# First block's two mixers: long convolution's taps all as matrix products from stored diagonals, output projection row by row into four PSUM banks

## Chip, cores and metric

The kernel runs on one core of a Trainium2 chip. The metric is the device time of one execution, from the first to the last instruction with the launch around it, in microseconds (us). Lower is better.

## What is computed

A network of two parts on 256 tokens of width 1024, in float32. The first block has two layers; each is a hybrid mixer, a residual sum with a layer norm, a feed-forward net (dense in layer 0, a mixture of eight experts in layer 1) and another layer norm. A second block with three kinds of attention and two more feed-forward nets follows; the change leaves it alone. What matters here, cut from the reference:

```python
def hybrid_mixer(...):
    proj = jnp.einsum('btd,de->bte', x, w_in)
    ...
    o_a = (rms_norm_f32(o_a, gdn_norm_w) * silu(a_gate)) ...    # 384 columns, gated delta rule
    glu_a, glu_b = jnp.split(c_glu, 2, axis=-1)
    u = glu_a * jax.nn.sigmoid(glu_b)
    u = causal_depthwise_conv(u, cnv_dw_w) + cnv_dw_b           # 31 taps, 256 channels
    o_b = jax.nn.silu(layer_norm(u, cnv_ln_g, cnv_ln_b))
    ...                                                         # o_c: 384 columns, attention
    mixed = jnp.concatenate([o_a, o_b, o_c], axis=-1) * mix_scale
    return jnp.einsum('bte,ed->btd', mixed, w_out)              # 1024 x 1024

x = layer_norm(DEEPNORM_ALPHA * x + mix, ln_mix_g[l], ln_mix_b[l])
```

## The kernel before

Tokens stand in two tiles of 128, channels in chunks of 128. Matrix products with weights are done in three pieces to keep float32 accuracy: `load` (L166) fetches a weight block of 1 MB into one of four `raw` buffers, `part` (L169) splits each half of it into a high part `wh` (a copy on ScalarE, L172) and a low part `wl` (a subtraction on VectorE, L174), three such pairs being held at a time, and `mm3` issues three products (L183 to L185) of a faster float32 form. `split_t` transposes activations on TensorE (L267) and splits them in the same way (L277, L278 with a gain). All other products are plain float32 products at L362; the profile shows each of those as two instructions.

`mixer1` (L354) is one layer's mixer. Its last part runs five generators: the inverse of the delta rule's triangular blocks, the `scan` over four chunks of 64 tokens (`g_ws`, `g_S`, `g_o`), the attention `fox` (`f_fl` logits, `f_fpt` transposes, `f_fo` values), `conv`, and `gates`. They are written one after another, but a scheduler that works with its own estimate of every instruction's time sets the order in which the instructions stand on each engine; an engine then works through its own list in that order. PSUM has eight banks: two under the tag `a`, four under `g`, two under `f`.

`conv` (L740) builds the gated input `up` (`cup`, 30 zeros and 256 tokens for each of two channel chunks) and applies 31 taps to each chunk. The nearest 6 taps of a chunk (8 in layer 1) go to TensorE: ScalarE scales the identity by the tap's weights (`dgt`, L756) and a product with it adds the shifted input to the bank `a_conv`. The other 25 (23) are one VectorE instruction each (L762, L764), which multiplies a shifted input by the weights and adds to `ccv`. L765 adds both. Then comes a layer norm over channels, with two products with ones (`f_cmean`, `f_cvar`), and a SiLU (L771 to L784).

`gates` (L787) projects the last 256 gate columns (48 products into `a_pB`), and applies a SiLU in three ScalarE passes. After the five, the convolution's result is scaled and split into chunks 3 and 4 of `mT` (L802, L803), the attention's result is transposed into chunks 5 to 7, and the delta rule's, normed and gated (L810 to L816), into chunks 0 to 2.

The output projection (L823 to L828) takes the 1024 output columns in four blocks of 256. Each block loads all 1024 rows of its columns, sums 48 products of 256 columns into one bank (`proj_b`), and is added to the residual (L826) with its statistics taken (L828), while TensorE goes on with the next block. `moments` (L834) then joins the statistics of both token tiles, takes the reciprocal root on ScalarE, and `layer_norm_T` or `layer_norm_T_first` scales (L850, L851 or L864) and transposes.

Of the kernel before, what the change touches and what calls it, by code (L numbers as in the profile page):

```python
# [9 lines left out]
F32 = mybir.dt.float32  # L10
# [4 lines left out]
AF = mybir.ActivationFunctionType  # L15
ALU = mybir.AluOpType
# [64 lines left out]
FOXC, GLUC = (5, 6, 7), (8, 9)  # L81

PCOLS1 = []
for _l in range(2):
    PCOLS1 += [(f"rowp{_l}", 24), (f"cw{_l}", 36), (f"mix{_l}", 8), (f"gnw{_l}", 1), (f"dww{_l}", 62), (f"dwb{_l}", 2),
               (f"clg{_l}", 2), (f"clb{_l}", 2)]
# [17 lines left out]
class Net:  # L104
# [249 lines left out]
    def mixer1(self, l, x, xT):  # L354
# [6 lines left out]
        def mm(out, lhsT, rhs, start=True, stop=True, **kw):  # L361
            PE.matmul(out, lhsT, rhs, start=bool(start), stop=bool(stop), skip_group_check=True, **kw)  # L362
# [377 lines left out]
        def conv():  # L740
# [9 lines left out]
            near = 31 - (6, 8)[l]  # L750
            dw, db = self.col1(f"dww{l}"), self.col1(f"dwb{l}")
            pc = self.ps("a", "conv").rearrange("p (c n) -> p c n", c=2)
            for c in range(2):
                for j in range(near, 31):
                    dg = mp.tile([P, P], F32, name="dgt", bufs=2)
                    S.activation(dg, ident, AF.Copy, scale=dw[:, c * 31 + j:c * 31 + j + 1])  # L756
                    mm(pc[:, c, :], dg, up[:, c, j:j + T], start=j == near, stop=j == 30)
            for c in range(2):
                for j in range(near):
                    w = dw[:, c * 31 + j:c * 31 + j + 1]  # L760
                    if j == 0:
                        V.tensor_scalar(cv[:, c, :], up[:, c, 0:T], w, db[:, c:c + 1], op0=ALU.mult, op1=ALU.add)  # L762
                    else:
                        V.scalar_tensor_tensor(cv[:, c, :], up[:, c, j:j + T], w, cv[:, c, :], op0=ALU.mult, op1=ALU.add)  # L764
            V.tensor_tensor(cv, cv, pc, op=ALU.add)  # L765
            yield
            ps = self.ps("f", "cmean")
# [5 lines left out]
            ps = self.ps("f", "cvar")  # L773
# [26 lines left out]
        for c in range(2):  # L800
            g = msc[:, 3 + c:4 + c]
            S.activation(mT[0][:, 3 + c, :], cv[:, c, :], AF.Copy, scale=g)  # L802
            V.scalar_tensor_tensor(mT[1][:, 3 + c, :], cv[:, c, :], g, mT[0][:, 3 + c, :].bitcast(F32),  # L803
                                   op0=ALU.mult, op1=ALU.subtract)
        self.split_t("f", mixed, mT, range(5, 8), gains=msc, src0=3)
# [12 lines left out]
        self.dump(f"cv{l}", cv)  # L818


        self.split_t("g", mixed, mT, range(0, 3), gains=msc, src0=0)
        r, st = x, self.new_stats()
        for c in range(4):  # L823
            ps = self.proj_b(A["w_out"][l, c], mT)
            s = slice(c * 256, c * 256 + 256)
            V.scalar_tensor_tensor(r[:, :, s], x[:, :, s], ALPHA, ps, op0=ALU.mult, op1=ALU.add)  # L826
            for t in range(2):
                V.bn_stats(out=st[:, t, c, :], in_=r[:, t, s])  # L828
# [5 lines left out]
    def moments(self, r, st, n):  # L834
        nc = self.nc
        mv, rs = self.ap.tile([P, 2, 2], F32, name="bnmv"), self.ap.tile([P, 2], F32, name="bnrs")
        for t in range(2):
            nc.vector.bn_aggr(out=mv[:, t, :], in_=st[:, t, :n, :])
        self.normed = self.rsqrt(rs, mv[:, :, 1], 1.0, 1e-5)
        return mv, rs  # L840

    def layer_norm_T(self, tag, r, st, rows, n=4):

        V = self.nc.vector
        mv, rs = self.moments(r, st, n)
        xT = self.new_xT()
        for h in range(2):
            s = slice(h * 512, h * 512 + 512)
            for t in range(2):
                V.scalar_tensor_tensor(r[:, t, s], r[:, t, s], mv[:, t, 0:1], rows[:, 0, s], op0=ALU.subtract, op1=ALU.mult)  # L850
                V.scalar_tensor_tensor(r[:, t, s], r[:, t, s], rs[:, t:t + 1], rows[:, 1, s], op0=ALU.mult, op1=ALU.add)  # L851
            self.split_t(tag, r, xT, range(4 * h, 4 * h + 4), src0=4 * h)
        return xT

    def layer_norm_T_first(self, tp, tag, r, st, rows, name, n=4):
# [3 lines left out]
        mv, rs = self.moments(r, st, n)  # L859
        hi, lo = xT = self.new_xT()  # L860
        for h in range(2):
            s = slice(h * 512, h * 512 + 512)
            for t in range(2):
                V.tensor_scalar(r[:, t, s], r[:, t, s], mv[:, t, 0:1], rs[:, t:t + 1], op0=ALU.subtract, op1=ALU.mult)  # L864
# [917 lines left out]
def zeros(*s):  # L1782
    return np.zeros(s, np.float32)


def pack_first(I):
# [6 lines left out]
    out["w_out"] = pack_b(I["w_out"])  # L1793
    cols = {}
    for l in range(2):
# [7 lines left out]
        cols[f"dww{l}"] = I["cnv_dw_w"][l].reshape(31, 2, P).transpose(2, 1, 0).reshape(P, 62)  # L1803
# [54 lines left out]
def build(tc, A, out):  # L1858
    with ExitStack() as ctx:
# [14 lines left out]
        with net.banks(a=2, g=4, f=2), pool("mix1") as net.mp:  # L1874
            rows = net.load_rows(net.mp.tile([P, 2, D], F32, name="rows", tag="lb"), "ln_ffn", 0, 2)
            xT = net.layer_norm_T("g", r, st, rows, 2)
            r, st = net.mixer1(1, r, xT)
# [36 lines left out]
```

## Time and profile before

| | us |
|---|---|
| median of 3 runs | 2170.08 (2164.84 to 2173.29) |
| the profiled execution, its own time | 2177.81 |
| span of its instructions | 2176.0 |
| first mixer's last part, projection included | about 118 to 207 |
| second mixer's last part, projection included | about 521 to 616 |

Times below count from the start of the span. The clock of TensorE is given as a share of its full 2.4 GHz: 1.00, or 0.50 for 1.2 GHz. A matrix product's listed duration holds its way through the array, so successive products overlap; what one costs in a row of them is the distance from start to start.

### The profile page before, as it was taken

The numbers are of one execution on the slowest core, as the hardware profiler recorded it, in microseconds if no ns is written. First come the engines' busy times: TensorE is split into PE (matmuls) and PEld (weight loads), VectorE is DVE, ScalarE is ACT, GpSimd is POOL, SyncE is SP. The second block draws the span as 40 slices with busy tenths as digits, with TensorE's granted clock in tenths as the row PEclk, the third lists the DMA queues.
The fourth block names the chain that finished last, engine by engine and source line by source line (L and its number), as shares of the span: only waits on it lengthen the run. The fifth ranks groups of instructions, "written<-read, shape, count | busy, mean of one in ns | idle before, by whom it ended". The sixth has DMA issues, their size and how long they took to land. (4 is left out here: it accounts for less than half of the span.)

```text
span 2176.0 us, 31850 instructions
## 1 busy us (share of the span) xinstructions
PE 2079.3 (96%) x12770; PEld 1598.7 (73%) x12770; DVE 1295.8 (60%) x1903; ACT 1017.1 (47%) x1445; POOL 12.7 (1%) x27
## 2 busy tenths in 40 slices
PE   8998999899979999999999999999899999999998
PEld 7887999778766565565565565555699988888997
DVE  6767955676666555454564465454555568765444
ACT  6545444464435454444454454443444444644443
POOL 0000000000000000000000000000000000000000
PEclk9979999998889999999999999999999999999999
DMA  6313675422359999999999999999455553444552
GB/s 236 104 44 118 213 258 182 137 90 96 139 178 347 364 406 378 415 415 371 401 372 383 400 389 393 421 417 398 168 192 180 190 183 126 136 164 155 186 183 98
DMA packets 78987, 545.36 MB, mean 251 GB/s; under 512 B 8960, under 2 KB 11272, under 8 KB 13936
## 3 DMA queue, kind: packets, MB, share of 16 engines
q1 hardware_dynamic: 76112, 527.40, 63.8%
q0 software_dynamic: 2720, 15.84, 2.0%
q8 instruction: 103, 1.69, 0.3%
q14 instruction: 52, 0.43, 0.1%
HBM read 536.72 MB, written 6.49 MB: 250 GB/s over the span
## 5 line engine op out<-in xcount | busy, mean ns | idle before, releaser
L174 DVE TENSOR_TENSOR wl<-raw,wh 128x1024 fp32r<-128x1024 f32 (+1 forms) x662 | 798.1, 1217 | 432.3 <-ACT wh L172 420.5
L172 ACT ACTIVATE wh<-raw 128x1024 fp32r<-128x1024 f32 (+1 forms) x662 | 690.7, 1054 | 627.9 <-PE a_pA L184 270.3
L183 PE MATMUL a_pA<-xTh,wh 128*128 128x256 f32 x1456 | 419.0, 289 | 6.2 <-ACT foxqk L620 3.5
L185 PE MATMUL a_pA<-xTh,wl 128*128 128x256 f32 x1456 | 415.5, 286 | 0.8 <-DVE wl L174 0.7
L184 PE MATMUL a_pA<-xTl,wh 128*128 128x256 f32 x1456 | 415.6, 286 | 0.4 <-DVE xTl L278 0.2
L183 PEld LDWEIGHTS a_pA<-xTh,wh 128*128 128x128 f32 x1456 | 280.8, 193 | 14.7 <-ACT foxqk L620 5.6
L184 PEld LDWEIGHTS a_pA<-xTl,wh 128*128 128x128 f32 x1456 | 281.0, 193 | 5.3 <-issue 3.2
L185 PEld LDWEIGHTS a_pA<-xTh,wl 128*128 128x128 f32 x1456 | 280.8, 193 | 3.8 <-issue 2.2
L1033 PE MATMUL a_up<-raw,xef 128*64 128x512 f32 x896 | 213.5, 596 | 0.0
L184 PE MATMUL a_up<-wl,xeh 128*128 128x512 f32 x448 | 180.7, 403 | 0.5 <-DVE wl L174 0.4
L183 PE MATMUL a_up<-wh,xeh 128*128 128x512 f32 x448 | 177.7, 400 | 0.0
L185 PE MATMUL a_up<-wh,xel 128*128 128x512 f32 x448 | 177.3, 396 | 0.0
L1033 PEld LDWEIGHTS a_up<-raw,xef 128*64 128x64 f32 x896 | 65.1, 137 | 127.8 <-issue 122.3
L1038 DVE TENSOR_TENSOR mos<-mos,a_up 128x512 f32<-128x512 f32 x42 | 28.8, 685 | 200.3 <-PE a_up L1033 149.8
L183 PE MATMUL a_pB<-wh,xTh 128*128 128x256 f32 x480 | 141.5, 296 | 5.7 <-ACT glu L620 3.2
L185 PE MATMUL a_pB<-wh,xTl 128*128 128x256 f32 x480 | 138.6, 291 | 1.6 <-DVE xTl L278 1.6
L184 PE MATMUL a_pB<-wl,xTh 128*128 128x256 f32 x480 | 139.8, 292 | 0.0
L1066 PE MATMUL y_y<-raw,mof 128*64 128x512 f32 x448 | 132.8, 602 | 0.7 <-ACT mof L1052 0.7
L184 PEld LDWEIGHTS a_up<-wl,xeh 128*128 128x128 f32 x448 | 84.6, 189 | 34.5 <-issue 11.4
L183 PEld LDWEIGHTS a_up<-wh,xeh 128*128 128x128 f32 x448 | 84.7, 189 | 28.1 <-ACT wh L172 7.3
L185 PE MATMUL acc_acc<-wh,ffl 128*128 128x512 f32 x264 | 102.0, 392 | 0.0
L184 PE MATMUL acc_acc<-wl,ffh 128*128 128x512 f32 x264 | 101.9, 392 | 0.0
(556 smaller groups left out, 2703.2 us busy)
## 6 DMA issues: line engine op xcount, KB each, us to landing
raw<-in_moe_w_dram SPq DMA_DIRECT2D x336, 1024.0 KB, 9.2
raw<-in_ffn_in_dram SPq DMA_DIRECT2D x44, 1024.0 KB, 4.9
raw<-in_ffn_w_dram SPq DMA_DIRECT2D x33, 1024.0 KB, 5.0
raw<-in_w_in_a_dram SPq DMA_DIRECT2D x24, 1024.0 KB, 4.9
raw<-in_ffn_out_dram SPq DMA_DIRECT2D x22, 1024.0 KB, 4.9
raw<-in_w_out_dram SPq DMA_DIRECT2D x12, 1024.0 KB, 4.9
raw<-in_w_in_g_dram SPq DMA_DIRECT2D x12, 1024.0 KB, 4.9
raw<-in_w_in_b_dram SPq DMA_DIRECT2D x6, 1024.0 KB, 5.1
```

The costliest lines, as they stand in the source:

```text
L172: nc.scalar.activation(wh[:, :m], raw[:, o:o + m], AF.Copy)
L174: nc.vector.tensor_tensor(wl[:, :m], raw[:, o:o + m], wh[:, :m].bitcast(F32), op=ALU.subtract)
L183: mm(out, lh, rh, start=start, stop=False, skip_group_check=True)
L184: mm(out, lh, rl, start=False, stop=False, skip_group_check=True)
L185: mm(out, ll, rh, start=False, stop=stop, skip_group_check=True)
L1033: PE.matmul(ps[r], xe[0][:, k0, r], w[:, k * 512:k * 512 + 512], start=k0 == 0, stop=k0 == 7, skip_group_check=True)
L1038: V.tensor_tensor(s, s, pp[1], op=ALU.mult)
L1066: PE.matmul(py[h][r], hf[:, k, r], w[:, j * 1024 + h * 512:j * 1024 + h * 512 + 512], start=b == 0 and k == 0, stop=b == 6 and k == 3, ski ...
```

## The change

All 62 taps of a layer become products on TensorE. Their diagonal matrices are no longer made on the chip: they are prepared beforehand as `w_tap`, four blocks of 1 MB per layer, which go through the same four `raw` buffers as the weights. The VectorE and ScalarE instructions of the taps are gone; the bias is added by two ScalarE copies out of PSUM. The two products of the channel norm take `g` banks in place of `f`. The output projection runs by rows of the weight matrix: a block of 1 MB holds two chunks of 128 rows in all 1024 columns, in the order 5, 6, 7, 3, 4, 0, 1, 2, and each chunk's products, now 512 columns wide, go to four banks that stay open (two token tiles by two column halves). The source writes the last three chunks bank by bank, and the statistics, the root and the scaling token tile by token tile; the second layer's mixer enters through the changed `layer_norm_T` too.

```diff
@@ -79,10 +79,11 @@
+OUT_ROWS = [5, 6, 7, 3, 4, 0, 1, 2]
...
@@ -747,30 +748,23 @@
             V.memset(up[:, :, 0:30], 0.0)
             V.tensor_tensor(up[:, :, 30:], glu[:, 2:4, :], sg, op=ALU.mult)
             yield
-            near = 31 - (6, 8)[l]
-            dw, db = self.col1(f"dww{l}"), self.col1(f"dwb{l}")
+            db = self.col1(f"dwb{l}")
             pc = self.ps("a", "conv").rearrange("p (c n) -> p c n", c=2)
+            for i in range(4):
+                raw = self.load(A["w_tap"][l, i]).rearrange("p (j n) -> p j n", n=P)
+                for n in range(16 * i, min(16 * i + 16, 62)):
+                    c, j = n // 31, n % 31
+                    mm(pc[:, c, :], raw[:, n % 16, :], up[:, c, j:j + T], start=n == 0, stop=n == 61)
             for c in range(2):
-                for j in range(near, 31):
-                    dg = mp.tile([P, P], F32, name="dgt", bufs=2)
-                    S.activation(dg, ident, AF.Copy, scale=dw[:, c * 31 + j:c * 31 + j + 1])
-                    mm(pc[:, c, :], dg, up[:, c, j:j + T], start=j == near, stop=j == 30)
-            for c in range(2):
-                for j in range(near):
-                    w = dw[:, c * 31 + j:c * 31 + j + 1]
-                    if j == 0:
-                        V.tensor_scalar(cv[:, c, :], up[:, c, 0:T], w, db[:, c:c + 1], op0=ALU.mult, op1=ALU.add)
-                    else:
-                        V.scalar_tensor_tensor(cv[:, c, :], up[:, c, j:j + T], w, cv[:, c, :], op0=ALU.mult, op1=ALU.add)
-            V.tensor_tensor(cv, cv, pc, op=ALU.add)
-            yield
-            ps = self.ps("f", "cmean")
+                S.activation(cv[:, c, :], pc[:, c, :], AF.Identity, bias=db[:, c:c + 1])
+            yield
+            ps = self.ps("g", "cmean")
             for c in range(2):
                 mm(ps[:, :T], self.ones, cv[:, c, :], start=c == 0, stop=c == 1)
             for c in range(2):
                 V.scalar_tensor_tensor(cv[:, c, :], ps[:, :T], -1.0 / 256, cv[:, c, :], op0=ALU.mult, op1=ALU.add)
             S.activation(csq, cv, AF.Square)
-            ps = self.ps("f", "cvar")
+            ps = self.ps("g", "cvar")
             for c in range(2):
                 mm(ps[:, :T], self.ones, csq[:, c, :], start=c == 0, stop=c == 1)
             crs = glu[:, 2, :]
@@ -797,12 +791,6 @@
         V.tensor_scalar(msc[:, 0:3], msc[:, 0:3], self.col1(f"gnw{l}"), None, op0=ALU.mult)
         self.emit(inverse(), scan(), fox(), conv(), gates())
         mT = self.new_xT()
-        for c in range(2):
-            g = msc[:, 3 + c:4 + c]
-            S.activation(mT[0][:, 3 + c, :], cv[:, c, :], AF.Copy, scale=g)
-            V.scalar_tensor_tensor(mT[1][:, 3 + c, :], cv[:, c, :], g, mT[0][:, 3 + c, :].bitcast(F32),
-                                   op0=ALU.mult, op1=ALU.subtract)
-        self.split_t("f", mixed, mT, range(5, 8), gains=msc, src0=3)
 
 
         for t in range(2):
@@ -816,52 +804,73 @@
             V.tensor_tensor(mixed[:, t, 0:384], sq, o_sb[:, t, :], op=ALU.mult)
         self.dump(f"mixed{l}", mixed)
         self.dump(f"cv{l}", cv)
-
-
         self.split_t("g", mixed, mT, range(0, 3), gains=msc, src0=0)
+
+
+        self.split_t("g", mixed, mT, range(5, 8), gains=msc, src0=3)
+        for c in range(2):
+            g = msc[:, 3 + c:4 + c]
+            S.activation(mT[0][:, 3 + c, :], cv[:, c, :], AF.Copy, scale=g)
+            V.scalar_tensor_tensor(mT[1][:, 3 + c, :], cv[:, c, :], g, mT[0][:, 3 + c, :].bitcast(F32),
+                                   op0=ALU.mult, op1=ALU.subtract)
+        acc = [self.ps(n, "wo") for n in "ffaa"]
+        last = []
+
+        def out(k, w, t, h, **kw):
+            ts, hs = slice(t * P, t * P + P), slice(h * 512, h * 512 + 512)
+            self.mm3(acc[2 * t + h], mT[0][:, k, ts], mT[1][:, k, ts], w[0][:, hs], w[1][:, hs], **kw)
+
+        for i in range(4):
+            for k, w in zip(OUT_ROWS[2 * i:2 * i + 2], self.weights(A["w_out"][l, i])):
+                if k < 3:
+                    last.append((k, w))
+                    continue
+                for t in range(2):
+                    for h in range(2):
+                        out(k, w, t, h, start=k == OUT_ROWS[0], stop=False)
         r, st = x, self.new_stats()
-        for c in range(4):
-            ps = self.proj_b(A["w_out"][l, c], mT)
-            s = slice(c * 256, c * 256 + 256)
-            V.scalar_tensor_tensor(r[:, :, s], x[:, :, s], ALPHA, ps, op0=ALU.mult, op1=ALU.add)
-            for t in range(2):
-                V.bn_stats(out=st[:, t, c, :], in_=r[:, t, s])
+        for t in range(2):
+            for h in range(2):
+                for k, w in last:
+                    out(k, w, t, h, start=False, stop=k == OUT_ROWS[-1])
+                s = slice(h * 512, h * 512 + 512)
+                V.scalar_tensor_tensor(r[:, t, s], x[:, t, s], ALPHA, acc[2 * t + h], op0=ALU.mult, op1=ALU.add)
+                V.bn_stats(out=st[:, t, h, :], in_=r[:, t, s])
         return r, st
 
     def new_stats(self):
         return self.ap.tile([P, 2, 4, 6], F32, name="bnst")
 
-    def moments(self, r, st, n):
-        nc = self.nc
+    def moments(self, st):
+
         mv, rs = self.ap.tile([P, 2, 2], F32, name="bnmv"), self.ap.tile([P, 2], F32, name="bnrs")
         for t in range(2):
-            nc.vector.bn_aggr(out=mv[:, t, :], in_=st[:, t, :n, :])
-        self.normed = self.rsqrt(rs, mv[:, :, 1], 1.0, 1e-5)
-        return mv, rs
-
-    def layer_norm_T(self, tag, r, st, rows, n=4):
+            self.nc.vector.bn_aggr(out=mv[:, t, :], in_=st[:, t, :2, :])
+            self.normed = self.rsqrt(rs[:, t:t + 1], mv[:, t, 1:2], 1.0, 1e-5)
+            yield t, mv[:, t, 0:1], rs[:, t:t + 1]
+
+    def layer_norm_T(self, tag, r, st, rows):
 
         V = self.nc.vector
-        mv, rs = self.moments(r, st, n)
         xT = self.new_xT()
-        for h in range(2):
-            s = slice(h * 512, h * 512 + 512)
-            for t in range(2):
-                V.scalar_tensor_tensor(r[:, t, s], r[:, t, s], mv[:, t, 0:1], rows[:, 0, s], op0=ALU.subtract, op1=ALU.mult)
-                V.scalar_tensor_tensor(r[:, t, s], r[:, t, s], rs[:, t:t + 1], rows[:, 1, s], op0=ALU.mult, op1=ALU.add)
-            self.split_t(tag, r, xT, range(4 * h, 4 * h + 4), src0=4 * h)
+        for t, mv, rs in self.moments(st):
+            for h in range(2):
+                s = slice(h * 512, h * 512 + 512)
+                V.scalar_tensor_tensor(r[:, t, s], r[:, t, s], mv, rows[:, 0, s], op0=ALU.subtract, op1=ALU.mult)
+                V.scalar_tensor_tensor(r[:, t, s], r[:, t, s], rs, rows[:, 1, s], op0=ALU.mult, op1=ALU.add)
+                if t:
+                    self.split_t(tag, r, xT, range(4 * h, 4 * h + 4), src0=4 * h)
         return xT
 
-    def layer_norm_T_first(self, tp, tag, r, st, rows, name, n=4):
+    def layer_norm_T_first(self, tp, tag, r, st, rows, name):
 
         V, S = self.nc.vector, self.nc.scalar
         g, b = self.col1(name + "g"), self.col1(name + "b")
-        mv, rs = self.moments(r, st, n)
         hi, lo = xT = self.new_xT()
-        for h in range(2):
-            s = slice(h * 512, h * 512 + 512)
-            for t in range(2):
-                V.tensor_scalar(r[:, t, s], r[:, t, s], mv[:, t, 0:1], rs[:, t:t + 1], op0=ALU.subtract, op1=ALU.mult)
+        for t, mv, rs in self.moments(st):
+            for h in range(2):
+                s = slice(h * 512, h * 512 + 512)
+                V.tensor_scalar(r[:, t, s], r[:, t, s], mv, rs, op0=ALU.subtract, op1=ALU.mult)
...
@@ -1790,7 +1799,11 @@
     out["w_in_a"] = pack_a(a)
     out["w_in_b"] = pack_b(w[:, :, W_IN_B])
     out["w_in_s"] = pack_b(w[:, :, W_IN_S], 18)[:, 0]
-    out["w_out"] = pack_b(I["w_out"])
+    taps = zeros(2, 64, P, P)
+    i = np.arange(P)
+    taps[:, :62, i, i] = I["cnv_dw_w"].reshape(2, 31, 2, P).transpose(0, 2, 1, 3).reshape(2, 62, P)
+    out["w_tap"] = np.ascontiguousarray(taps.reshape(2, 4, 16, P, P).transpose(0, 1, 3, 2, 4)).reshape(2, 4, P, 2048)
+    out["w_out"] = pack_rows(I["w_out"].reshape(2, KC, P, D)[:, OUT_ROWS].reshape(2, D, D))
     cols = {}
     for l in range(2):
         cw = I["gdn_conv_w"][l]
```

The order in which instructions now stand differs from the source in places. TensorE in the first mixer's last part, around the second chunk of the scan, before:

```order
L362 MATMUL g_ws<-late 64x128 x3
L362 MATMUL g_o<-late,kq_283 64x128
L362 MATMUL g_o<-late,kq_358 64x128
L362 MATMUL g_o<-late,kq_431 64x128
L362 MATMUL f_fo<-fv,fpT 128x64 x12
L362 MATMUL a_conv<-cup,dgt 128x256 x2
L362 MATMUL g_S<-late,kd_792 64x64 x2
L362 MATMUL g_S<-late,kd_799 64x64 x2
L362 MATMUL g_S<-late,kd_806 64x64 x2
```

The same engine from the third chunk of the scan to the first product of `gates`, now:

```order
L363 MATMUL g_o<-late,AT_537 64x64 x2
L363 MATMUL g_o<-late,AT_554 64x64 x2
L363 MATMUL g_o<-late,AT_571 64x64 x2
L363 MATMUL a_conv<-cup,raw 128x256 x11
L363 MATMUL g_ws<-late 64x128 x3
L363 MATMUL g_o<-late,kq_283 64x128
L363 MATMUL g_o<-late,kq_358 64x128
L363 MATMUL g_o<-late,kq_431 64x128
L363 MATMUL a_conv<-cup,raw 128x256 x11
L363 MATMUL g_o<-late,AT_537 64x64 x2
L363 MATMUL g_o<-late,AT_554 64x64 x2
L363 MATMUL g_o<-late,AT_571 64x64 x2
```

The taps stood singly or in pairs between the scan's steps, with the products of `gates` among them; now they stand in runs of up to 11 (3, 3, 3, 6, 1, 8, 10, 11, 11, 6 in either mixer), and all 48 products of `gates` come after the last run.

ScalarE in the first mixer, from the copy of the `gates` bank on, before (the channel norm's square is L772, its SiLU further down; L735 copies the scan's results):

```order
L790 ACTIVATE gate<-a_pB 128x2x256
L172 ACTIVATE wh<-raw 128x1024
L299 ACTIVATE late<-gate 128x768
L300 ACTIVATE late<-late,bias_294 128x768
L735 ACTIVATE mixed<-g_o 64x384
L301 ACTIVATE late<-late 128x768
L810 ACTIVATE late<-mixed 128x384
L772 ACTIVATE glu<-ccv 128x512
L293 ACTIVATE ors<-ors,bias_524 128x6
L735 ACTIVATE mixed<-g_o 64x384
```

The same engine now, further down in the same chain, as far as the first copies of transposed tiles (L813 scales the convolution's result, L278 splits the transposed tiles):

```order
L302 ACTIVATE late<-late 128x768
L798 ACTIVATE late<-mixed 128x384 x2
L300 ACTIVATE glu<-glu 128x512
L294 ACTIVATE ors<-ors,bias_524 128x6
L301 ACTIVATE glu<-glu,bias_294 128x512
L295 ACTIVATE ors<-ors 128x6
L294 ACTIVATE ors<-ors,bias_524 128x6
L302 ACTIVATE glu<-glu 128x512
L295 ACTIVATE ors<-ors 128x6
L813 ACTIVATE xTh<-ccv,msc 128x256 x2
L278 ACTIVATE xTh<-g_tr,msc 128x256 x6
```

The gate's SiLU stood among the scan's last copies; now it stands behind them, the convolution's SiLU follows it, and all six splits of transposed tiles stand behind both.

VectorE at the end of the first mixer's projection, before:

```order
L826 SCALAR_TENSOR_TENSOR x<-x,a_pB 128x2x256
L828 BN_STATS bnst<-x 128x6 x2
L174 TENSOR_TENSOR wl<-raw,wh 128x1024
L838 BN_AGGR bnmv<-bnst 128x2 x2
L864 TENSOR_SCALAR x<-x,bnmv,bnrs 128x512 x4
```

and now:

```order
L837 SCALAR_TENSOR_TENSOR x<-x,f_wo 128x512 x2
L837 SCALAR_TENSOR_TENSOR x<-x,a_wo 128x512 x2
L838 BN_STATS bnst<-x 128x6 x2
L175 TENSOR_TENSOR wl<-raw,wh 128x1024
L838 BN_STATS bnst<-x 128x6 x2
L848 BN_AGGR bnmv<-bnst 128x2 x2
L873 TENSOR_SCALAR x<-x,bnmv,bnrs 128x512 x4
```

Both token tiles' sums, statistics and roots stand side by side rather than one tile after the other. On TensorE the last chunks of rows stand chunk by chunk through all four banks (two products for one bank, two for the next), so that the four banks close within the last eight products.

## Rows read from the trace of the kernel before

**Rows 1.** The page's first part: busy us, share of the span, instructions.

```profile
PE 2079.3 (96%) x12770; PEld 1598.7 (73%) x12770; DVE 1295.8 (60%) x1903; ACT 1017.1 (47%) x1445; POOL 12.7 (1%) x27
```

**Rows 2.** First mixer by stretches: length, engines' busy us, TensorE's clock, DMA share, GB/s.

```profile
122.20:146.10 23.90, 23.90 (x191) 16.58 (x187) 12.90 (x38) 8.85 (x32) 0.00 (x0) 0.50 0.01 2
146.10:162.30 16.20, 16.20 (x150) 14.65 (x149) 13.74 (x33) 5.68 (x14) 0.00 (x0) 1.00 0.20 66
162.30:175.90 13.60, 9.02 (x81) 7.04 (x81) 10.79 (x23) 9.73 (x21) 0.87 (x2) 1.00 0.00 1
175.90:203.00 27.10, 26.44 (x192) 25.90 (x192) 19.16 (x35) 13.31 (x20) 1.19 (x3) 0.87 0.55 197
```

**Rows 3.** The second mixer in the same view; columns PE, PEld, DVE, ACT, POOL.

```profile
525.00:552.30 27.30, 27.30 (x210) 19.18 (x210) 14.01 (x41) 10.36 (x36) 0.00 (x0) 0.50 0.00 1
573.10:580.50 7.40, 4.81 (x33) 3.46 (x32) 5.92 (x14) 5.17 (x14) 0.49 (x1) 1.00 0.93 352
580.50:608.60 28.10, 25.82 (x192) 24.80 (x192) 14.63 (x26) 9.51 (x14) 0.04 (x1) 0.94 0.71 269
```

**Rows 4.** Taps on TensorE: the tile's view (ns min/median/max), then the timeline (start, us).

```profile
L362 PE MATMUL a_conv<-cup,dgt x56: 377/483/795, 123.0 to 571.3; 128*128 128x256 f32 x56
...
132.23 2.07 PE L362 MATMUL a_conv<-cup,dgt 128*128 128x256 f32 x4
...
149.92 1.03 PE L362 MATMUL a_conv<-cup,dgt 128*128 128x256 f32 x4
```

**Rows 5.** Taps on VectorE, and a VectorE instruction queued among them with its wait.

```profile
L764 DVE SCALAR_TENSOR_TENSOR ccv<-cup,p,ccv x92: 443/477/486, 122.6 to 565.4; 128x256 f32<-128x256 f32 x92
...
129.31 0.69 DVE L661 TENSOR_REDUCE fsx<-f_fl 128x2 f32<-128x512 f32 x1 [4.07 <-PE f_fl L362]
```

**Rows 6.** Timeline of ScalarE and VectorE behind the products of `gates` in the first mixer.

```profile
162.30 0.60 ACT L790 ACTIVATE gate<-a_pB 128x512 f32<-128x512 f32 x1 [2.76 <-PE a_pB L185]
162.79 1.05 ACT L172 ACTIVATE wh<-raw 128x1024 fp32r<-128x1024 f32 x1
163.74 0.83 ACT L299 ACTIVATE late<-gate 128x768 f32<-128x768 f32 x1
...
166.68 0.96 DVE L792 TENSOR_TENSOR gate<-gate,late 128x768 f32<-128x768 f32 x1 [0.27 <-ACT late L301]
...
177.77 0.71 ACT L300 ACTIVATE glu<-glu,bias 128x512 f32<-128x512 f32 x1
...
179.18 0.69 DVE L784 TENSOR_TENSOR ccv<-ccv,glu 128x512 f32<-128x512 f32 x1 [0.79 <-ACT glu L301]
...
179.90 0.91 ACT L802 ACTIVATE xTh<-ccv,msc 128x256 fp32r<-128x256 f32 x2 [0.76 <-DVE ccv L784]
```

**Rows 7.** Timeline of TensorE: 512-column products into four banks (20 starts between), 256-column ones (156).

```profile
254.83 0.39 PE L183 MATMUL acc_acc<-wh,ffh 128*128 128x512 f32 x1
...
259.37 0.39 PE L185 MATMUL acc_acc<-wh,ffl 128*128 128x512 f32 x1
...
184.01 0.28 PE L183 MATMUL a_pB<-wh,xTh 128*128 128x256 f32 x1
...
202.73 0.28 PE L185 MATMUL a_pB<-wh,xTl 128*128 128x256 f32 x1
```

**Rows 8.** Timeline of VectorE and TensorE at the first norm; statistics over 512 columns elsewhere.

```profile
203.04 0.69 DVE L826 SCALAR_TENSOR_TENSOR x<-x,a_pB 128x512 f32<-128x512 f32 x1 [0.56 <-PE a_pB L185]
203.76 0.75 DVE L828 BATCH_NORM_STATS2 bnst<-x 128x6 f32<-128x256 f32 x2
204.44 1.21 DVE L174 TENSOR_TENSOR wl<-raw,wh 128x1024 fp32r<-128x1024 f32 x1
...
206.54 1.92 DVE L864 TENSOR_SCALAR x<-x,bnmv,bnrs 128x512 f32<-128x512 f32 x4 [0.60 <-ACT bnrs L294]
...
207.14 3.70 PE L869 MATMUL a_tr<-call,x 128*128 128x128 f32 x16 [4.13 <-DVE x L864]
...
407.74 0.67 DVE L906 BATCH_NORM_STATS2 bnst<-x 128x6 f32<-128x512 f32 x1
```

More of the change, by code (lines that the diff above doesn't have):

```diff
@@ L81 @@
 FOXC, GLUC = (5, 6, 7), (8, 9)
+OUT_ROWS = [5, 6, 7, 3, 4, 0, 1, 2]
 PCOLS1 = []
 for _l in range(2):
-    PCOLS1 += [(f"rowp{_l}", 24), (f"cw{_l}", 36), (f"mix{_l}", 8), (f"gnw{_l}", 1), (f"dww{_l}", 62), (f"dwb{_l}", 2),
+    PCOLS1 += [(f"rowp{_l}", 24), (f"cw{_l}", 36), (f"mix{_l}", 8), (f"gnw{_l}", 1), (f"dwb{_l}", 2),
                (f"clg{_l}", 2), (f"clb{_l}", 2)]
@@ L1802, in pack_first @@
         cols[f"gnw{l}"] = np.concatenate([I["gdn_norm_w"][l]] * 2)[:, None]
-        cols[f"dww{l}"] = I["cnv_dw_w"][l].reshape(31, 2, P).transpose(2, 1, 0).reshape(P, 62)
         cols[f"dwb{l}"] = chan(I["cnv_dw_b"][l], 2)
@@ L1875, in build @@
             rows = net.load_rows(net.mp.tile([P, 2, D], F32, name="rows", tag="lb"), "ln_ffn", 0, 2)
-            xT = net.layer_norm_T("g", r, st, rows, 2)
+            xT = net.layer_norm_T("g", r, st, rows)
             r, st = net.mixer1(1, r, xT)
```

## The prediction

> **What bounds the kernel now.** Read the engine shares first [rows 1]: TensorE is busy for 96% of the span, so work that is added to it is suspected of lengthening the span until an idle or slowed stretch is found that takes it in. The change works in two places, the last parts of the two mixers, so the next view is the table of stretches for these [rows 2, 3]. It shows three things.
>
> First, from the start of the convolution to the end of the gate's products TensorE has no idle time at all: 23.90 of 23.90 us and 16.20 of 16.20 in the first mixer, 27.30 of 27.30 in the second. VectorE, which carries most of the taps, is busy for 12.90 of the 23.90 us. Second, in the two long stretches TensorE's granted clock is 0.50, that is 1.2 GHz, although it never rests: what it does there are attention logits with 18 and 64 rows and products of 32 and 64 rows and columns, with a few full-size taps among them. Third, in the stretch before the output projection TensorE idles, 13.60 - 9.02 = 4.58 us in the first mixer and 7.40 - 4.81 = 2.59 in the second, and within the projection 27.10 - 26.44 = 0.66 and 28.10 - 25.82 = 2.28 us.
>
> Is it VectorE that holds TensorE back in the long stretch? Then taking the taps away from it would pay. An instruction of the attention that is queued behind taps on VectorE shows the reverse [rows 5]: VectorE had finished its taps and stood idle for 4.07 us, waiting for TensorE's logits. So the last parts of the mixers are bound by TensorE, first by its work at either clock, then by the chain through ScalarE and VectorE that leads to the projection.
>
> **Taps.** 50 taps in the first layer and 46 in the second leave VectorE (0.48 us each [rows 5], hidden beside TensorE) and go to TensorE; 28 diagonals leave ScalarE, hidden too. A tap is two instructions there. One alone takes 0.377 us, four in a row 1.03, so each further one adds (1.03 - 0.377) / 3 = 0.218 us; at half clock (2.07 - 0.795) / 3 = 0.425 [rows 4]. A tap costs 0.436 us or 0.85. With no idle time around them 96 taps add 96 x 0.436 = 41.9 us, 21.8 and 20.1. This is the bulk of the sum. In the new order 9 taps stand ahead of the scan's first state product where 6 stood, so 3 more in either mixer fall into the slow stretch if that stays: 6 x 0.41 = 2.5 us, less what moves out of it; taken as 2.
>
> Is the long stretch still slow? The work that stands there keeps its shape; what is new is a run of three taps for every two or three logits. A run is 1.3 us at full clock, against some 2 to 4 us of small products around it. In the trace two pairs of taps in the same stretch did not lift the clock. I take it that the slow stretches stay about as long, and keep the other end (both vanish, less 23.90 / 2 + 27.30 / 2 = 25.6 us) as a rival.
>
> The Trainium skill, on the page "TensorE: Matmul & The Clock Gate", section "Loop structure matters more than you think", says that it is the loop nest that decides whether matmuls stay warm: issued back to back they keep the full clock. The trace differs here, since 23.90 us without a gap ran at 0.50 [rows 2]; by the page's rule that stretch would not be slow at all, before or after, and the time would be that of the rival "full clock" below.
>
> **The chain to the projection.** All 48 products of the gate now stand behind the last tap, and behind them on ScalarE comes everything that leads to `mT`. The durations are in the trace [rows 6]: copy of the bank 0.60, a weight split that stands next in the queue 1.05, three SiLU passes of at least 0.83 (2.49), VectorE's product 0.96; then, since the convolution's SiLU is queued behind and the transposed splits behind that, three passes of 0.71 (2.13), VectorE's product 0.69, the two scalings 0.91, the first split 0.46. Sum 9.3 us. Between them stand hand-overs and small instructions of the norm, for which I add 2 (from 0 to 4): 11.3 us from the last gate product to the first of the projection. TensorE fills some 2.4 of it (two products of the channel norm, 0.87 like two taps, and transposes), so it idles about 8.9 us. Before it was 4.58 and 2.59, since the gate's products stood between the scan's steps; that is +4.3 and +6.3. The late splits then no longer stall the projection: -0.66 and -2.28. Together +7.7 (from +4 to +13). Who waits for this chain is TensorE alone, with the whole projection queued.
>
> The tap blocks take the four `raw` buffers, so the gate's and the projection's loads start only as runs of taps end. The last of those loads to be needed, rows of the third block, starts at the last tap and has the chain and half the projection to arrive: nothing.
>
> **Projection.** It changes from 192 products of 256 columns to 96 of 512. Start to start these are (202.73 - 184.01) / 156 = 0.120 us and (259.37 - 254.83) / 20 = 0.227 us [rows 7]: 23.0 against 21.8 us, -1.2 each, -2.5 together. The clock dips at its start (0.87 and 0.94 [rows 2, 3]) because of the idle time ahead; this stays.
>
> [...]
>
> **Norm.** Before, 4.1 us pass from the last product to the first transposes (203.0 to 207.14 [rows 8]): one addition 0.69, statistics of two pieces 0.75, a weight split 1.21, the root, the scaling. The new order doesn't take one token tile ahead of the other: four banks close within 2 us, and then four additions (0.6 apart), four statistics of 0.67 and the same split stand in the queue, and the transposes need the third of four scalings (1.92 / 4 apart) instead of the second. That is about 2.8 us more by the rows, but additions and statistics may overlap the last products. I take +2 for each mixer, +4 (from -4, if the halves work as the source writes them, to +8).
>
> **Sum.** 41.9 + 2 + 7.7 - 2.5 + 4 = +53.1 us. The profiled execution of 2177.81 us would take 2231; it lies 7.7 us above the median of the runs, from which I count: 2170.08 + 53.1 = 2223.
>
> **Rivals.**
> *Full clock in the long stretches.* Runs of full-size taps among the logits keep TensorE at 2.4 GHz. For it: in 146.1 to 162.3, with taps and gate products among the same scan, the clock was 1.00 [rows 2]. Against it: 0.50 for 24 and 27 us with taps in them. Price -25.6 and -2: 2196; in one mixer only, about 2210.
>
> *The taps are absorbed: not slower.* TensorE's stream becomes so dense that the clock stays full from the logits to the norm and no idle time is left. The gain is at most 25.6, plus 0.13 x 27.1 + 0.06 x 28.1 = 5.2 in the projections, plus the idle 4.58 + 2.59 + 0.66 + 2.28 = 10.1: 40.9 us, against 41.9 - 2.5 = 39.4 of work. That gives -1.5, 2169. It decides only if all of this is gained; each half-clock stretch of 10 us that stays costs 5. Against it stands the new order, in which the gate's chain has nothing left on TensorE to cover it.
>
> *Bank cycling slows the projection.* The new products would run at half clock throughout, 0.227 x 96 = 21.8 us more in each mixer: 2267. The rows of the feed-forward net speak against it. [...]
>
> **How the numbers follow.** The forecast has 0.62, full clock in one or both long stretches 0.21, absorbed taps 0.08, bank cycling 0.03, something else 0.06. The range for 8 in 10 takes in the full-clock case and the forecast's own bounds: from 2223 - 27.6 - 10 = 2186 to 2223 + 15 = 2238. A measurement of this kernel can tell about 0.5% from no change, 11 us; only the absorbed case and part of the rest end within that, so faster 0.05, same 0.08, slower 0.87.
>
> **What would show it.** Right: DVE's tap instructions gone, `a_conv` with 248 instructions on TensorE at about 0.218 us from start to start in the long runs; a stretch of about 24 to 28 us at 0.50 in both mixers from the first logits on; the first projection product some 25 us later than before, counted from the logits, with TensorE idle 7 to 11 us before it; products of 0.227 us in `f_wo` and `a_wo`; 5 to 7 us from the last of them to the first transposes. Wrong: the clock at 1.00 through the logits, TensorE idle inside the runs of taps (a late tap block), or a projection that starts right behind the gate's last product.

## The result and the profile after

The changed kernel takes 2224.13 us (median of 4 executions, 2219.05 to 2232.37) where the kernel before takes 2169.47: a ratio of 1.0257, 95% interval 1.0219 to 1.0294. The forecast was 2223. Two later comparisons gave 1.0197 (1.0170 to 1.0223) and 1.0235 (1.0199 to 1.0272).

The page's first part, in answer to [rows 1]:

```profile
PE 2119.7 (95%) x12770; PEld 1628.1 (73%) x12770; DVE 1259.2 (56%) x1797; ACT 1011.6 (45%) x1427; POOL 12.8 (1%) x27
```

TensorE is busy 40.4 us longer, with the same number of instructions: 192 for taps came, 192 products of the projections went. VectorE lost 36.6 us of work, and the kernel is slower all the same.

Both mixers by stretches, in answer to [rows 2, 3] (length, then busy us of PE, PEld, DVE, ACT, POOL, TensorE's clock, DMA share, GB/s); of each mixer the stretch of the logits, the taps and gate products, the chain, and the projection:

```profile
121.50:152.20 30.70, 30.70 (x185) 21.47 (x185) 4.97 (x15) 6.85 (x26) 0.00 (x0) 0.50 0.01 1
152.20:196.20 44.00, 44.00 (x332) 38.60 (x332) 11.13 (x20) 9.69 (x16) 0.00 (x0) 1.00 0.36 120
196.20:208.20 12.00, 3.32 (x17) 2.86 (x16) 8.54 (x17) 9.51 (x20) 0.35 (x1) 0.66 0.26 87
208.20:231.20 23.00, 22.97 (x98) 18.63 (x96) 14.31 (x24) 11.60 (x17) 1.73 (x4) 0.96 0.66 232
...
551.60:578.00 26.40, 26.40 (x282) 19.68 (x283) 5.74 (x20) 9.92 (x37) 0.00 (x0) 0.87 0.01 2
578.00:621.50 43.50, 43.50 (x323) 38.26 (x315) 11.23 (x21) 9.69 (x16) 0.00 (x0) 1.00 0.35 122
621.50:633.40 11.90, 3.22 (x16) 2.76 (x15) 8.46 (x17) 9.45 (x20) 0.22 (x1) 0.72 0.94 376
633.40:657.10 23.70, 23.69 (x98) 19.18 (x97) 10.05 (x15) 8.28 (x12) 0.32 (x1) 0.93 0.67 241
```

TensorE has no idle time from the logits to the last gate product, so no tap block came late. The two mixers run the same list of instructions, yet among the logits the first ran at 0.50 throughout and the second at 0.87 on average. The chain costs 12 us in either, of which TensorE works 3.3.

Each part is bounded by products of TensorE; in the first mixer, before and then after, these are the inverse's first products, the first projection product and (after) the last one:

```profile
110.79 1.05 PE L362 MATMUL g_x<-u,NT 32*32 32x32 f32 x96
175.88 0.39 PE L183 MATMUL a_pB<-wh,xTh 128*128 128x256 f32 x1 [0.73 <-ACT xTh L277]
...
113.08 1.04 PE L363 MATMUL g_x<-u,NT 32*32 32x32 f32 x96
208.18 0.78 PE L184 MATMUL f_wo<-wh,xTh 128*128 128x512 f32 x1
230.79 0.39 PE L186 MATMUL a_wo<-wh,xTl 128*128 128x512 f32 x1
```

Measured between starts of products (us):

| | first mixer, before | after | second mixer, before | after |
|---|---|---|---|---|
| inverse's first 96 products to first projection product | 65.1 | 95.1 | 66.9 | 85.8 |
| first to last projection product | 26.8 | 22.6 | 27.8 | 23.2 |
| last projection product to the norm's first transposes | 4.4 | 7.4 | 5.4 | 9.8 |

That is +30.0 - 4.2 + 3.0 in the first mixer and +18.9 - 4.6 + 4.4 in the second, 47.5 us of the 2232.37 - 2177.81 = 54.6 between the two profiled executions. The other 7 lie outside these parts. Out there 14.9 us more than before ran at 0.50, which would be 6.5 at the price of slow clock found below (an estimate).

The taps in TensorE's timeline (20 instructions in a row) and in the tile's view, in answer to [rows 4]:

```profile
168.84 4.59 PE L363 MATMUL a_conv<-cup,raw 128*128 128x256 f32 x20
```

```profile
L363 PE MATMUL a_conv<-cup,raw x248: 377/379/742, 130.7 to 614.5; 128*128 128x256 f32 x124
```

From start to start a tap's instruction takes (4.59 - 0.377) / 19 = 0.222 us; the forecast had 0.218.

The chain behind the last gate product, in answer to [rows 6] (ScalarE, VectorE, then TensorE):

```profile
196.23 0.60 ACT L784 ACTIVATE gate<-a_pB 128x512 f32<-128x512 f32 x1 [1.20 <-PE a_pB L186]
196.72 1.05 ACT L173 ACTIVATE wh<-raw 128x1024 fp32r<-128x1024 f32 x1
...
203.60 0.71 ACT L301 ACTIVATE glu<-glu,bias 128x512 f32<-128x512 f32 x1
...
205.51 0.69 DVE L778 TENSOR_TENSOR ccv<-ccv,glu 128x512 f32<-128x512 f32 x1
...
195.91 0.28 PE L186 MATMUL a_pB<-wh,xTl 128*128 128x256 f32 x1
...
205.74 2.79 PE L268 MATMUL g_tr<-call,mixed 128*128 128x128 f32 x12 [8.68 <-DVE mixed L804]
```

The last gate product starts at 195.91, the first projection product at 208.18: 12.27 us, with one idle time of 8.68. The second mixer shows the same two numbers.

The projection, in answer to [rows 7]; between the starts of these two lie 76 steps from product to product:

```profile
212.43 0.39 PE L184 MATMUL f_wo<-wh,xTh 128*128 128x512 f32 x1
...
229.65 0.39 PE L185 MATMUL f_wo<-wl,xTh 128*128 128x512 f32 x1
```

17.22 / 76 = 0.227 us each, as in the feed-forward net. The first norm, in answer to [rows 8] (VectorE, then TensorE):

```profile
230.73 1.28 DVE L837 SCALAR_TENSOR_TENSOR x<-x,f_wo 128x512 f32<-128x512 f32 x2
231.92 1.28 DVE L837 SCALAR_TENSOR_TENSOR x<-x,a_wo 128x512 f32<-128x512 f32 x2
233.12 1.28 DVE L838 BATCH_NORM_STATS2 bnst<-x 128x6 f32<-128x512 f32 x2
234.31 1.21 DVE L175 TENSOR_TENSOR wl<-raw,wh 128x1024 fp32r<-128x1024 f32 x1
235.44 1.28 DVE L838 BATCH_NORM_STATS2 bnst<-x 128x6 f32<-128x512 f32 x2
...
238.17 3.29 PE L878 MATMUL a_tr<-call,x 128*128 128x128 f32 x16 [7.00 <-DVE x L873]
```

Four additions, four statistics and a weight split stand in one queue behind the last products, and TensorE waits 7.00 us.

### The profile page after: what moved, and what is told of

Read it like the earlier page. It is cut to its first block, busy times and chain, and to the rows that moved or that the text cites. A ratio compares the mean times of both kernels' runs of the same rounds, so it can differ in the third digit from the quotient of the medians.

```text
span 2230.6 us, 31743 instructions
## 1 busy us (share of the span) xinstructions
PE 2119.7 (95%) x12770; PEld 1628.1 (73%) x12770; DVE 1259.2 (56%) x1797; ACT 1011.6 (45%) x1427; POOL 12.8 (1%) x27
## 5 line engine op out<-in xcount | busy, mean ns | idle before, releaser
L1042 PEld LDWEIGHTS a_up<-raw,xef 128*64 128x64 f32 x896 | 65.1, 137 | 127.8 <-issue 122.1
L185 PEld LDWEIGHTS a_up<-wl,xeh 128*128 128x128 f32 x448 | 84.6, 189 | 35.0 <-issue 12.2
L184 PE MATMUL a_pB<-wh,xTh 128*128 128x256 f32 x352 | 101.9, 291 | 3.2 <-ACT glu L621 3.2
L185 PE MATMUL a_pB<-wl,xTh 128*128 128x256 f32 x352 | 101.8, 289 | 0.0
L186 PE MATMUL a_pB<-wh,xTl 128*128 128x256 f32 x352 | 101.3, 288 | 0.0
```

The lines of the kernel that those rows point to most:

```text
L184: mm(out, lh, rh, start=start, stop=False, skip_group_check=True)
L185: mm(out, lh, rl, start=False, stop=False, skip_group_check=True)
L186: mm(out, ll, rh, start=False, stop=stop, skip_group_check=True)
L1042: PE.matmul(ps[r], xe[0][:, k0, r], w[:, k * 512:k * 512 + 512], start=k0 == 0, stop=k0 == 7, skip_group_check=True)
```

## The experiments

**The changed kernel twice more.** No edit.

> The changed kernel itself, for a second profiled execution. Theory C1 (the order of the instructions settles the clock): 0.50 in the same places as in its first trace, one stretch of about 31 us in the first mixer from the attention's logits on, none over 7 us among the logits of the second mixer. Theory C2 (the same order can run at either clock): at least one of the two stretches differs by over 10 us from the first trace, in either direction. Time 2219 to 2235 by either; what stands still between the two executions, work and waits at full clock, should agree within 1 us in each mixer.

> The changed kernel a third time, in more rounds. Theory C2 (the same order runs at either clock, from execution to execution): times spread over at least 10 us, in step with each execution's mean granted clock (2211 at 0.974, 2219 at 0.971, 2232 at 0.966 so far), with the median between those of the first two comparisons, 1.020 to 1.026 times the kernel before. Theory G (the two comparisons differed by the chip they ran on): spread under 6 us, at one of the two ratios. In the trace, from the inverse's first products to the first projection product 81 to 82 us where no slow stretch falls in, and 0.44 us more for each us of slow clock there.

Measured 2214.08 us (2211.12 to 2223.11) against 2173.68, and 2224.80 (2209.52 to 2232.50) against 2171.20. Stretches of the second trace (first mixer's logits; its taps and gate products; second mixer's inverse and logits), then of the third (first mixer's logits; its taps):

```profile
122.00:136.00 14.00, 14.00 (x157) 9.57 (x158) 3.56 (x13) 5.42 (x21) 0.00 (x0) 1.00 0.01 2
136.00:179.50 43.50, 43.50 (x328) 38.26 (x320) 11.29 (x21) 9.66 (x16) 0.00 (x0) 1.00 0.36 121
524.00:555.50 31.50, 31.10 (x510) 24.47 (x512) 10.29 (x35) 13.68 (x48) 0.00 (x0) 1.00 0.11 36
```

```profile
124.00:144.50 20.50, 20.50 (x132) 13.80 (x130) 3.50 (x13) 5.57 (x21) 0.00 (x0) 0.50 0.01 2
144.50:188.00 43.50, 43.50 (x329) 38.05 (x328) 11.13 (x20) 9.69 (x16) 0.00 (x0) 1.00 0.36 121
```

Among the logits one list of instructions ran at 0.50 for 30.7, 0 and 20.5 us in the first mixer, and for 6.9, 0 and 6.9 in the second. C2 holds, C1 and G fall: the third comparison alone spread over 23 us. From the inverse to the projection the first mixer took 95.1, 81.6 and 90.7 us, which prices slow clock among the logits at (95.1 - 81.6) / 30.7 = 0.44 us for each us. The rest stood still: the wait before the norm was 7.38 and 9.79 in all three.

**The convolution alone.** The kernel before, with

```diff
-            near = 31 - (6, 8)[l]
...
+            for i in range(4):
+                raw = self.load(A["w_tap"][l, i]).rearrange("p (j n) -> p j n", n=P)
```

> The kernel before with one part of the change, all 62 taps of a layer on TensorE from stored diagonals; projection by column blocks and norm as before. Theory A (the terms of the sum are separate, and the convolution carries the slowdown): 41.9 us of taps, 2 more in the slow stretch, and 7.7 of the longer chain to the projection, less 2.9 of late splits: 51 to 54 us more, 2221 to 2224; if the second mixer's long stretch at 0.50 goes, as in the changed kernel's trace (27.3 us to 6.9), 10 less, 2211 to 2214. The first projection product then starts about 30 (19 to 30 in the second mixer) us later after the inverse's first full-set product than before. Rival B (the projection into four open banks and the new norm order carry a good part, and the taps fill slow or idle stretches): under 35 us more, below 2205.

2235.30 us (2226.45 to 2238.07) against 2173.65, ratio 1.0293 (1.0264 to 1.0321). B falls: the convolution carries more than the whole slowdown. A had 51 to 54 us more and 61.7 came, so A is 8 to 11 us short. In the trace the first mixer took 85.0 us from inverse to projection with 3.4 of slow clock, close to the changed kernel's 81.6 without any; in the second the scheduler made another order (35.5 us from the inverse's first products to the first tap, 16.3 in the changed kernel), the stretch of 27.3 us at 0.50 came back, and it took 98.6. A part of the shortfall shows there: from inverse to projection TensorE idles 10.5 and 12.4 us, against 8.7 and 9.1 in the second trace of the changed kernel, and the second norm's transposes come 7.6 us after the last product (5.4 before).

**Half of the taps.** The changed kernel, leaving out every second tap:

```diff
-                for n in range(16 * i, min(16 * i + 16, 62)):
+                for n in range(16 * i, min(16 * i + 16, 62), 2):
```

> The changed kernel with every second tap left out, 62 taps of 124 in all; the convolution is incomplete. Theory A (each tap lies on the path at 0.436 us): 27 us less than the changed kernel, within 5 us for the clock. Rival B (a part of the taps only fills slow or idle time): at most 15 us less.

2204.30 us (2199.05 to 2209.95): 9.8 less than the changed kernel beside it, which by itself would speak for B. The trace shows why not; its slow stretches in the two mixers, where the second trace above had none:

```profile
123.80:144.30 20.50, 20.50 (x132) 13.78 (x130) 3.49 (x13) 5.54 (x21) 0.00 (x0) 0.50 0.01 2
533.40:567.50 34.10, 34.10 (x225) 24.43 (x223) 4.97 (x15) 8.48 (x32) 0.00 (x0) 0.50 0.01 1
```

From inverse to projection it took 77.3 and 84.1 us. Less 0.44 x 20.5 = 9.0 and 0.44 x 34.1 = 15.0 that is 68.3 and 69.1, against 81.6 and 82.2: 13.3 and 13.1 us for 31 taps, 0.43 and 0.42 each. A's price holds. In the two traces slow clock takes back 24.0 of these 26.4 us; the other executions have no trace, but their mean clocks point the same way, 0.962 to 0.968 against 0.970 to 0.974 for the changed kernel beside it.

**The gate first.** The changed kernel with

```diff
-        self.emit(inverse(), scan(), fox(), conv(), gates())
+        self.emit(inverse(), scan(), fox(), gates(), conv())
```

> The changed kernel with the gate's generator written ahead of the convolution's, so that the 48 gate products stand among the input projections and not behind the last tap. Theory A (behind the gate's products a chain of ScalarE and VectorE work keeps TensorE waiting 8.7 us in each mixer): the last tap is followed after 7 to 8 us by the first projection product, in place of 19.0, of which 6.6 were gate products; 4 to 6 us less in each mixer, 8 to 12 less than the changed kernel of the same comparison. Rival D (the convolution's own norm is the chain, and the gate stands beside it): 0 to 3 us less.

2209.52 us (2195.03 to 2211.91), ratio 1.0142 (1.0110 to 1.0175) where the changed kernel beside it had 1.0197. TensorE behind the last taps of the first mixer:

```profile
183.72 3.62 PE L363 MATMUL a_conv<-cup,raw 128*128 128x256 f32 x16
187.90 1.13 PE L363 MATMUL g_cmean<-ccv,ones 128*128 128x256 f32 x4 [0.56 <-ACT ccv L759]
190.54 1.13 PE L363 MATMUL g_cvar<-glu,ones 128*128 128x256 f32 x4 [1.51 <-ACT glu L766]
191.51 1.47 PE L268 MATMUL g_tr<-call,mixed 128*128 128x128 f32 x12
```

The idle time of 8.68 is gone, and 0.56 and 1.51 stand in its place; 6.75 us pass from the last tap to the first projection product in both mixers, where 18.96 did. Of these 12.2 us less, 6.6 are gate products, which now stand elsewhere; the other 5.6 in each mixer are A's, where D had at most 3 in all. A holds in the trace. The time shows 4.6 of the 8 to 12 us between medians, with slow stretches of 23.9 and 24 us in this trace against none in the other's.

**Projection and norm without the taps.** `rows_only` is the changed kernel with `conv` of before:

```diff
-            for i in range(4):
-                raw = self.load(A["w_tap"][l, i]).rearrange("p (j n) -> p j n", n=P)
...
+            near = 31 - (6, 8)[l]
```

`rows_joint` is that with the joint root and scaling of before; `norm_only` is the kernel before with the reverse of this edit:

```diff
-            self.normed = self.rsqrt(rs[:, t:t + 1], mv[:, t, 1:2], 1.0, 1e-5)
+        self.normed = self.rsqrt(rs, mv[:, :, 1], 1.0, 1e-5)
```

`bank2` adds to `rows_only` an order that the scheduler must keep:

```diff
-                if k < 3:
+                if k in (1, 2):
...
+                with self.tc.issue_after(before.ins) if before else nullcontext():
```

> The changed kernel with the convolution of the kernel before: only the projection by rows and the norm half by half are new. Theory A: projection 4.2 and 4.6 us shorter as in the changed kernel's trace (or 1.2 each, if that came from the longer chain ahead of it), norm 3.0 and 4.4 longer: between -2 and +5 us, 2168 to 2175, no difference that can be measured. Rival B: at least 12 us slower, 2182 or more.

> As the kernel before with the projection by rows alone: the norm is joint again (one root and one set of statistics for both token tiles, scaling by column halves). Theory N1 (the longer wait before the norm's transposes comes from four banks that close together): it stays near 7.4 and 9.8 us from the last projection product, and the time is within 2 us of that with the norm half by half. Theory N2 (it comes from the order token tile by token tile): it falls back to 4.4 and 5.4 us, and the time to 2161 to 2168, 7 us below that with the norm half by half.

> The kernel before with the norm token tile by token tile alone (root and scaling of the first tile ahead of the second's); projection by column blocks, convolution as before. Theory N1: 4.4 and 5.4 us from the last projection product to the first transposes as before, time within 2 us of before. Theory N2: 7 and 9 to 10 us, time 6 to 8 us above before, 2176 to 2178.

> The projection by rows and the norm token tile by token tile with the convolution of the kernel before, and the last two chunks' products held to the order of the source, bank by bank, so that the banks close 1.4 us apart. Theory N1 (four banks that close within 2 us make the longer wait): from the last projection product to the norm's transposes 3.5 to 5 us in the first mixer and 5 to 6.5 in the second, in place of 9.0 and 9.6 without this order; the projection itself stays at about 22.2 us. 7 to 9 us less than with the chunks in turn, 2164 to 2168, that is 0.2% to 0.5% faster than the kernel before. Rival E (other work in VectorE's queue, such as the next weights' splits, sets the wait): it stays above 8 us, and the time at 2172 to 2178.

| | median us, ratio (95%) | projection | wait before the transposes |
|---|---|---|---|
| `rows_only` | 2176.37, 1.0017 (0.9999 to 1.0034) | 22.2, 22.1 | 9.0, 9.6 |
| `rows_joint` | 2174.78, 1.0007 (0.9990 to 1.0023) | 22.2, 22.1 | 9.1, 9.6 |
| `norm_only` | 2173.27, 1.0007 (0.9992 to 1.0023) | 25.4, 25.7 | 4.3, 5.5 |
| `bank2` | 2173.38, 1.0001 (0.9988 to 1.0014) | 22.2, 24.1 | 6.3, 5.5 |

N1 holds for the cause: the wait comes with the projection by rows, whichever way the norm is written, and shrinks where the banks close in turn. In the first mixer of `bank2` it stays above N1's 3.5 to 5 us, and E has a share, two splits that stand ahead of the last statistics:

```profile
195.09 2.36 DVE L175 TENSOR_TENSOR wl<-raw,wh 128x1024 fp32r<-128x1024 f32 x2
197.36 1.28 DVE L848 BATCH_NORM_STATS2 bnst<-x 128x6 f32<-128x512 f32 x2
...
199.23 1.12 PE L888 MATMUL a_tr<-call,x 128*128 128x128 f32 x4 [5.95 <-DVE x L883]
```

The 7 to 9 us that `bank2` was to gain over `rows_only` are 3.0 between medians, of two comparisons. In the traces 2.0 went to the second mixer's projection (24.1 against 22.1), where 4.2 us of slow clock fell on products, against 1.1; the rest stays open.

**All taps on VectorE.** `pe00` is the kernel before with

```diff
-            near = 31 - (6, 8)[l]
+            near = 31 - (0, 0)[l]
...
-            V.tensor_tensor(cv, cv, pc, op=ALU.add)
```

`best00` adds `bank2`'s projection with

```diff
-OUT_ROWS = [5, 6, 7, 3, 4, 0, 1, 2]
+OUT_ROWS = [5, 6, 7, 0, 1, 2, 3, 4]
```

and `best33` is that with `(3, 3)[l]`.

> The other way round: the kernel before with all 62 taps of a layer on VectorE and none on TensorE (no diagonals). Theory A (a tap costs 0.436 us where TensorE never rests and nothing where VectorE has room): 28 taps less, 12.2 us less than before, 2159 to 2164, 0.4% to 0.7% faster. VectorE's busy time in the 40 us from the scan's start to the end of the gate's products rises from 26.6 to about 32. Rival F (VectorE becomes late): the channel norm waits for the last tap and TensorE idles for it, no gain or a loss; the idle time ahead of the norm's products or of the projection grows by more than 3 us in each mixer.

> All taps on VectorE as in the run above, the projection by rows with the convolution's two chunks last (rows in the order 5, 6, 7, 0, 1, 2, 3, 4) and closed bank by bank, the norm token tile by token tile. Theory A: the 12.2 us of the taps and 3 us of each projection (22.2 us against about 25.5 by column blocks): 2153 to 2160, 0.6% to 0.9% faster than before. Rival F: the last taps are late, but the projection's first six chunks hide up to 16 us of that, so still 2160 to 2168.

> As the run above, with the three nearest taps of a channel chunk left on TensorE, 12 taps in all. Theory A: 16 taps less than before, 7.0 us, and 6 of the projections: 2158 to 2164, 5 us behind the run above. Rival F: VectorE has more room here, and this one is ahead of the run above.

`pe00`: 2168.87 us, ratio 0.9984 (0.9972 to 0.9997), a third of the 12.2. First mixer, the 40 us that the expectation names, and TensorE's idle time ahead of the transposes:

```profile
122.00:162.00 40.00, 38.70 (x362) 31.26 (x362) 33.38 (x88) 16.28 (x43) 0.00 (x0) 0.72 0.09 28
```

```profile
169.07 0.66 PE L267 MATMUL g_tr<-call,mixed 128*128 128x128 f32 x2 [4.80 <-DVE mixed L809]
```

VectorE is busy for 33.4 us, where 32 were forecast, and TensorE now idles 1.3 among it. From inverse to projection TensorE idles 7.3 and 7.1 us, where it idled 4.6 and 2.9 before: that takes back 7.0 of the 12.2 us, and the second mixer's wait before the norm's transposes another 2.2 (7.6 against 5.4). F has about the growth (2.7 and 4.2 us, with 3 as its mark), but not its cause: the wait that is shown ends with the gated result of the delta rule (`mixed`), and the channel norm's first product waited 0.38 us for the last tap in the first mixer and not at all in the second. `best00`: 2163.33 us, ratio 0.9949 (0.9930 to 0.9968), the fastest kernel here (only it and `pe00` have an interval below 1), with 59.1 and 60.4 us from inverse to projection. `best33`: 2175.98, ratio 1.0019 (1.0005 to 1.0033), with 65.2 and 65.3. That is 12.7 us behind `best00`, where A had 5 and F had it ahead. In its trace TensorE idles 7.1 us from inverse to projection in both mixers (5.3 and 4.1 in `best00`), and the second mixer's wait before the transposes is 7.5 us against 3.2; six taps are 2.6 by A's price. Why three taps of a chunk bring these waits was not tested.

## Why the prediction was right, step by step

**Taps: right.** TensorE had no room, and each tap cost 0.42 to 0.44 us (`half_taps`, and 0.222 for each of its two instructions in the trace).

**Chain: right.** 11.3 us and 8.9 idle were forecast, 12.27 and 8.68 came, and `gates_first` took the idle time away. Taps and chain together, with slow clock taken out at 0.44: 65.1 - 0.44 x 23.9 = 54.6 and 66.9 - 0.44 x 27.3 = 54.9 before, 81.6 and 82.2 in the second trace of the changed kernel. That is +27.0 and +27.3, forecast 21.8 + 4.3 and 20.1 + 6.3.

**Projection: mis-sized.** 1.9 and 3.5 us less were forecast with the late splits, 4.2 and 4.6 came. The 0.227 us was right. The step that failed is "this stays": in the first mixer the slow clock now falls mostly into the idle time ahead (200.0 to 210.2, of which 8.2 before the first product), where it costs 1.3 us on twelve transposes (2.79 against 1.47 in `gates_first`), while before 6.8 us of it lay on products. The longer chain by itself brings the larger part: `conv_only`, by column blocks, takes 23.9 and 25.4 us. In the second mixer slow clock on the products is the same, 3.4 us before and after, and why 1.1 us more was saved there stays open.

**Norm: mis-sized, cause right.** +3.0 and +4.4 in place of +2 each, by the queue that the forecast described; `norm_only` shows that the order token tile by token tile does nothing by itself. The two misses cancel: the projection by rows gives back to the norm nearly what it saves, and `rows_only` is level with before.

**Slow stretches: wrong as a fixed thing.** The forecast took them as staying, 24 to 28 us in both mixers, and gave "full clock" as a rival. The first trace had 30.7 and 6.9 us; the second trace had none, which the prediction names as a sign of being wrong. Both came, from execution to execution of one kernel. In the first trace they gave +3.0 and -9.0 us against before (6.8 more, 20.4 less, at 0.44), and 7 came in elsewhere, where the forecast had nothing. So the nearness of 2224 to 2223 is partly luck: the three medians are 2214 to 2225. The rival's price was 27.6 us; the first and second profiled executions, whose logits lie 37.6 us of slow clock apart, differ by 2232.37 - 2211.12 = 21.3. With full clock in both mixers the rival had 2196, and 2211.12 came. (The lower end of the range, 2223 - 27.6 - 10, is 2185 and not 2186.)

**Bank cycling: did not come.** The products ran at 0.227 us. The Trainium skill ("TensorE: Matmul & The Clock Gate", "A second HAM failure mode: psum-queue depth-cycling") tells of a kernel that cycled through PSUM banks with 512-column products and lost throughput because TensorE idled briefly between groups of products. Here TensorE was busy for 22.97 of the projection's 23.00 us, so no run of this case tests that.

**Absorbed taps: did not come.** No idle time was there to take them in, and even the second trace, all at full clock among the logits, is 33 us above the profiled execution before.

## What to carry to other kernels

Where one engine has no idle time, price every instruction moved to it from start to start and believe the sum. Take work off that engine, as `best00` does, but look at what is then left to cover its waits: `pe00` kept a third of what it took off. Whoever closes several accumulators together queues all that follows them on the next engine: close them in turn, and look at the order that the scheduler made, not at the source. Before two kernels are compared by one trace, take the clock out of both.

## What was not expected of the hardware

The granted clock of a stretch is not settled by the order of the instructions. In the first mixer of the changed kernel TensorE had the same list and no idle time from the inverse to the chain in all three traces, and ran among the logits at 0.50 or 1.00. (In the second mixer it idles once, 0.4 to 1.0 us, some 2 us behind the inverse's first products.) With the convolution of before, the first mixer's stretch was 23.9 us in five traces of five (`before`, `rows_only`, `rows_joint`, `norm_only`, `bank2`); in the changed kernel's three, 30.7, 0 and 20.5. In the second mixer it was 13.7 to 27.3 in those five. An execution's time follows its mean granted clock: in the third comparison the changed kernel took 2209.5 us at 0.975, 2224.7 at 0.969 and 2232.5 at 0.964. What tips a stretch one way or the other stays open.
